# Expert weights of a mixture-of-experts layer: gate and up in steps of 1,024 columns over two PSUM banks, down with four consecutive rows to a partition

## The chip, the cores and the metric

The kernel runs on one core of a Trainium2 chip. The metric is the device time of one execution in microseconds (us); lower is better. The core has a matrix engine (TensorE: PE for its matrix products, PEld for the loads of its stationary operand), three engines for element-wise work (VectorE or DVE, ScalarE or ACT, GpSimd or POOL), and SyncE (SP), which here only issues DMA transfers. SBUF is the working memory with 128 partitions; PSUM, in eight banks of 128 x 512 floats, takes the results of PE.

## The reference, cut to what matters

The reference is two stacked networks over 256 tokens of 1,024 features in float32. The last stage, which takes more than half of the time, is a mixture of eight experts. Each token goes to its two best experts:

```python
for e in range(N_EXPERTS):                       # 8 experts
    h = jax.nn.silu(x @ w_gate[e]) * (x @ w_up[e])
    out = out + gates[..., e:e + 1] * (h @ w_down[e])
```

`w_gate[e]` and `w_up[e]` are 1,024 x 3,584, `w_down[e]` is 3,584 x 1,024. All three are float32, so the eight experts have 352 million bytes of weights (336 pieces of 2^20 bytes).

## The kernel before, in words

**Weights.** All weights go through one class, `Stream` (line 66). A unit is a piece of 128 partitions x 2,048 floats, 1 MB. `plan_experts` (line 1564) lists the units in the order of their use, and `_load` (line 90) issues one DMA on SP's queue for the next unit as soon as a raw buffer is free. In the expert stage there are some eleven raw buffers in several rings. `_split` (line 105) turns a unit into two float32r tiles: ACT casts it to the high part `wH` (line 122), and DVE subtracts that to get the low part `wL` (line 123). There are three buffers of `wH` and three of `wL`, and `get` (line 141) hands one unit over and splits up to two further ones ahead. A raw buffer is free again when DVE has read it.

**Products.** Each float32 product is made of three float32r ones, `mm3` (line 229, its matmuls are lines 231 to 233): high by high, high by low, low by high. The tokens of an expert are at most 128 slots, gathered into `xg[e]` (tiles of the tags `xg`, `hT` and `hH` in turn); they are the stationary operand, and 512 columns of a weight are the moving one.

**A step.** `experts` (line 1387) runs over 8 experts and 7 steps of 512 of the 3,584 columns. In a step, `up` (line 1403) makes the gate product (two units, 24 matmuls into one bank of the PSUM tag `mm`), ACT's silu of it into the tile `mh` (line 1406), the up product (two units, 24 matmuls, another bank of `mm`), and DVE's product of the two (line 1410). Then `down` (line 1422) multiplies the step before with two units of the down weight (24 matmuls into the two accumulator banks of the expert), and `turn` (line 1413) transposes the new `mh` in four pieces on PE (line 1416) into a bank of `mm` and splits the result into `mhH` (ACT, line 377) and `mhL` (DVE, line 380). `mm` has four banks, the accumulators another four (lines 1654 and 1655); `mh` has one buffer, `mhH` and `mhL` two each. One step is 72 matmuls of 512 columns and four transposes, on six units.

**What happens between experts.** After the first step of an expert, `y_parts` and `y_split` (lines 1455 and 1458) split the sum of the expert before into `hL`, two halves of 512. In its second step `slots_back` (line 1462) brings them back to the tokens with eight matmuls into four banks of `mm`, and `add_back` (line 1474) adds them to the output on DVE. During experts 1, 3 and 5 the tokens of the next two experts are gathered by `gather_steps` (line 1350): four calls with eight matmuls into one bank of `mm` each (line 1368) and four small splits, and a fifth with four matmuls (line 1379), in the steps n = 2 to 6:

```python
if e % 2 and e < N_EXP - 1 and n >= 2:
    if n == 2:
        steps = self.gather_steps([e + 1, e + 2], base)
    out = next(steps)
```

**Order.** The kernel's source gives priorities in program order; the framework's list scheduler then fixes one order for every engine ahead of the run, where an instruction that is not ready lets a later one pass, and assigns the buffers. The order within an engine does not change while the kernel runs. Loads are kept in program order.

**Weight loads.** A gate or up unit is four blocks of 128 rows by 512 columns (`u_k4n512`, line 164), so each partition receives four runs of 2 KB. A down unit is two blocks of 128 rows by all 1,024 columns (`u_k2n1024`, line 179), two runs of 4 KB to each partition.

Of the kernel before, what the change touches and what calls it, by code (L numbers as in the profile page):

```python
# [7 lines left out]
F32R = mybir.dt.float32r  # L8
I32 = mybir.dt.int32
AF = mybir.ActivationFunctionType  # L10
ALU = mybir.AluOpType
# [3 lines left out]
P = 128  # L15
DM = 1024
# [4 lines left out]
D_FF = 2816  # L21
N_EXP = 8
D_EXP = 3584

C_ID, C_INV, C_NH, C_EARLY = 0, 128, 130, 146
C_STRIU, C_IOTA, C_TIE, C_ID32, C_MAIN = 146, 274, 530, 594, 626
# [137 lines left out]
def u_k4n512(w, k0, n0, loads=1):  # L164
    def f(dst):
        m = 4 // loads
        return [(w[(k0 + k) * P:(k0 + k + m) * P, n0:n0 + 512].rearrange("(k p) n -> p k n", p=P),
                 dst[:, k * 512:(k + m) * 512].rearrange("p (k n) -> p k n", k=m)) for k in range(0, 4, m)]
    return f
# [6 lines left out]
    return f  # L176


def u_k2n1024(w, k0):
    def f(dst):  # L180
        return [(w[k0 * P:(k0 + 2) * P, :].rearrange("(k p) n -> p k n", p=P),
                 dst.rearrange("p (k n) -> p k n", k=2))]
    return f


# [7 lines left out]
class Kern:  # L193
# [1072 lines left out]
    def route(self, tt):  # L1266

        nc, c = self.nc, self.c
        mask, pos = self.rt
        if tt == 0:  # L1270
            self.logits = self.few(self.wr, N_EXP, self.mp, self.pair_end)
        l = self.rl[:, tt, :]
        tmp = self.t(self.mp, [P, 512], "mh", bufs=1)
        gt, eq = [tmp[:, i:i + 64].rearrange("p (i j) -> p i j", i=8) for i in (0, 64)]
        o = nc.vector.tensor_copy(l, self.logits[:, tt * 8:(tt + 1) * 8])
        if tt:
            self.tc.keep_in_program_order(o)
            self.behind(o, self.st.last[1])
        pin = self.tc.keep_in_program_order
        tie = c[:, C_TIE:C_TIE + 64].rearrange("p (i j) -> p i j", i=8)  # L1280
        lj = l[:, None, :].to_broadcast([P, 8, 8])
        li = l[:, :, None].to_broadcast([P, 8, 8])
        pin(nc.vector.tensor_tensor(eq, lj, li, op=ALU.is_equal))
        pin(nc.vector.tensor_tensor(eq, eq, tie, op=ALU.mult))
        pin(nc.vector.tensor_tensor(gt, lj, li, op=ALU.is_gt))
# [101 lines left out]
    def experts(self, st, base):  # L1387

        nc = self.nc
        mp = self.mp  # L1390
        xg, y = {}, {}

        def product(w, e):
            ps = self.mm()
            for kh in range(2):
                H, L = st.get(f"m{w}{e}")
                for kk in range(4):
                    k = kh * 4 + kk
                    s = slice(kk * 512, kk * 512 + 512)
                    self.mm3(ps, xg[e][0][:, k, :], xg[e][1][:, k, :], H[:, s], L[:, s], k == 0, k == 7)  # L1400
            return ps

        def up(e, n, dense, between):
            h = self.t(mp, [P, 512], "mh", bufs=1)
            if dense is None:
                nc.scalar.activation(h, product("g", e), AF.Silu)
                between()
            else:
                dense_gather(h, dense)
            nc.vector.tensor_tensor(h, h, product("u", e), op=ALU.mult)  # L1410
            return h

        def turn(h):
            ps = self.mm()
            for j in range(4):
                nc.tensor.transpose(ps[:, j * P:(j + 1) * P], h[:, j * P:(j + 1) * P], self.ident)
            H = self.t(mp, [P, 512], "mhH", F32R, bufs=2)
            L = self.t(mp, [P, 512], "mhL", F32R, bufs=2)
            self.split_to(H, L, ps)
            return H, L  # L1420

        def down(e, n, HL):
            aH, aL = HL
            if n == 0:
                y[e] = [self.acc() for _ in range(2)]
            for u in range(2):
                H, L = st.get(f"md{e}")
                for nh in range(2):
                    for kk in range(2):
                        a = slice((2 * u + kk) * P, (2 * u + kk + 1) * P)  # L1430
                        s = slice(kk * DM + nh * 512, kk * DM + nh * 512 + 512)
                        self.mm3(y[e][nh], aH[:, a], aL[:, a], H[:, s], L[:, s],
                                 n == 0 and u == 0 and kk == 0, n == 6 and u == 1 and kk == 1)

        def down_last(e, HL):

            yHL = y_parts()
            stats = [self.t(self.sp, [P, 2, 6], "bnst", bufs=4) for _ in range(2)]
            for nh in range(2):
                H, L = st.get(f"md{e}")  # L1440
                for kk in range(4):
                    if nh and kk == 3:
                        ps = slots_back(e, 0, yHL)
                    a, s = slice(kk * P, (kk + 1) * P), slice(kk * 512, (kk + 1) * 512)
                    self.mm3(y[e][nh], HL[0][:, a], HL[1][:, a], H[:, s], L[:, s], False, kk == 3)
# [41 lines left out]
        def dense_parts(ps):  # L1487
            HLs = []
            for tt in range(2):
                h = self.t(mp, [P, 512], "mh", bufs=1)  # L1490
                nc.scalar.activation(h, ps[tt], AF.Silu)
                HLs.append([self.t(mp, [P, 512], "mh" + c, F32R, bufs=2) for c in "HL"])
                self.split_to(*HLs[tt], h)
            return HLs

        def dense_gather(h, HLs):

            ps = self.mm()
            for tt in range(2):
                for i in range(2):  # L1500
                    nc.tensor.matmul(ps, self.oh[:, tt, 0, :], HLs[tt][i], start=tt + i == 0, stop=tt + i == 2)
            nc.scalar.copy(h, ps)

        dense = None
        if base == 0:
# [16 lines left out]
            rv = None  # L1522
        st.pieces = 1
        prev = None
        for e, n in [(e, n) for e in range(N_EXP) for n in range(7)]:
            if prev is None:
                h = up(e, n, dense, lambda: None)
                prev = (e, n, None, h)
                continue
            if prev[2] is None:  # L1530
                h0 = prev[3]
                turned = []
                h = up(e, n, None, lambda: turned.append(turn(h0)))
                prev = (0, 0, turned[0])
            else:
                h = up(e, n, None, lambda: None)
            if e and n == 1:
                for nh in range(2):
                    add_back(e - 1, nh, slots_back(e - 1, nh, yHL))
            down(*prev)  # L1540
            with self.soon(60 if st.i >= len(st.units) - 2 else 0):
                prev = (e, n, turn(h))
            if e and n == 0:
                yHL = y_parts()
                for nh in range(2):
                    y_split(e - 1, nh, yHL)
            if e % 2 and e < N_EXP - 1 and n >= 2:
                if n == 2:
                    steps = self.gather_steps([e + 1, e + 2], base)
                out = next(steps)  # L1550
                if out:
                    xg[e + 1], xg[e + 2] = out
        return rv, down_last(N_EXP - 1, prev[2])

    def rest(self):

# [7 lines left out]
    def plan_experts(self, st):  # L1564
        a = self.a
        wg, wu, wd = a["moe_w_gate_2"][0], a["moe_w_up_2"][0], a["moe_w_down_2"][0]

        def dn(e, n):
            for u in range(2):
                st.add(f"md{e}", u_k2n1024(wd[e], n * 4 + 2 * u))  # L1570

        def dn_last(e, n):
            for nh in range(2):
                st.add(f"md{e}", u_k4n512(wd[e], n * 4, nh * 512, nh + 1))

        prev = None
        for e in range(N_EXP):
            for n in range(7):
                for c, w in (("g", wg), ("u", wu)):
                    for kh in range(2):  # L1580
                        st.add(f"m{c}{e}", u_k4n512(w[e], 4 * kh, n * 512))
# [238 lines left out]
```

## Time and profile before

| what | us |
|---|---|
| median of 3 runs (1815.80 to 1818.71) | 1817.25 |
| the profiled execution | 1815.42 |
| its span, first to last instruction | 1813.3 |

The profile is of one execution. Its page gives busy time by engine, then the span in 40 slices, then groups of instructions; a matmul's duration there includes the time in which it overlaps its neighbours, so the distance between the starts of two matmuls is what one of them costs. The expert stage begins at about 820 us of the span and PE's last matmul is near 1799 us; a layer norm and the output follow to 1813 us. A wait is put down to the engine or the DMA whose semaphore came last.

### The profile page before, as it was taken

How to read it: one execution, taken by the hardware profiler on the slowest of the kernel's cores; microseconds unless marked ns; L12 is line 12 of the kernel's file. 1: busy time of each engine (PE TensorE's matmuls, PEld its weight loads, DVE VectorE, ACT ScalarE, POOL GpSimd, SP SyncE). 2: the span in 40 equal slices, each digit the busy share in tenths (PEclk: the TensorE clock that was granted, in tenths of full speed). 3: DMA queues.
4: the chain of work that ended last, by engine and by line, in shares of the span. 5: the costliest groups of instructions: out<-in, count | busy, mean ns of one | idle time of the engine just before them, and what ended most of it. 6: DMA issues, size and time to landing. Idle time of an engine off the chain costs nothing. (4 is left out here: it accounts for less than half of the span.)

```text
span 1813.3 us, 24175 instructions
## 1 busy us (share of the span) xinstructions
PE 1755.9 (97%) x9653; PEld 1476.9 (81%) x9653; DVE 1435.7 (79%) x1453; ACT 1064.9 (59%) x1008; POOL 74.7 (4%) x116
## 2 busy tenths in 40 slices
PE   6999999999999999999999999999999999999996
PEld 3888767889689998977888888888878888888885
DVE  3899576569775557679889899888898898888887
ACT  3334344646343333347777777777777767677674
POOL 1010013002100001000000000000000000000000
PEclk9999999999999999999999999999999999999998
DMA  9988445249265557547999999999999999999991
GB/s 349 318 305 311 161 152 179 66 132 309 68 201 192 183 191 251 174 158 295 358 363 364 357 356 359 372 360 358 345 343 375 372 347 355 349 368 369 355 370 47
DMA packets 252615, 509.34 MB, mean 281 GB/s; under 512 B 12347, under 2 KB 68782, under 8 KB 251470
## 3 DMA queue, kind: packets, MB, share of 16 engines
q1 hardware_dynamic: 249550, 500.64, 78.0%
q0 software_dynamic: 2592, 6.97, 1.2%
q8 instruction: 78, 1.28, 0.3%
q14 instruction: 43, 0.35, 0.1%
q10 hardware_dynamic: 352, 0.10, 0.0%
HBM read 504.28 MB, written 1.05 MB: 279 GB/s over the span
## 5 line engine op out<-in xcount | busy, mean ns | idle before, releaser
L123 DVE TENSOR_TENSOR wL<-raw,wH 128x2048 fp32r<-128x2048 f32 (+2 forms) x582 | 1032.3, 1799 | 193.2 <-ACT wH L122 187.7
L122 ACT CAST wH<-raw 128x2048 fp32r<-128x2048 f32 (+2 forms) x582 | 870.0, 1520 | 410.3 <-PE mm L232 128.0
L231 PE MATMUL mm<-hH,wH 128*128 128x256 f32 x816 | 231.8, 284 | 0.0
L232 PE MATMUL mm<-hL,wH 128*128 128x256 f32 x816 | 231.6, 284 | 0.0
L233 PE MATMUL mm<-hH,wL 128*128 128x256 f32 x816 | 231.2, 283 | 0.0
L231 PE MATMUL mm<-wH,hH 128*128 128x512 f32 (+1 forms) x512 | 197.1, 387 | 5.7 <-ACT wH L122 2.6
L232 PE MATMUL mm<-wL,hH 128*128 128x512 f32 (+1 forms) x512 | 197.6, 386 | 2.6 <-DVE wL L123 2.5
L232 PE MATMUL acc<-wL,mhH 128*128 128x512 f32 x448 | 176.8, 395 | 0.0
L233 PE MATMUL acc<-wH,mhL 128*128 128x512 f32 x448 | 174.7, 390 | 0.0
L231 PE MATMUL acc<-wH,mhH 128*128 128x512 f32 x448 | 162.6, 390 | 0.0
L231 PEld LDWEIGHTS mm<-hH,wH 128*128 128x128 f32 x816 | 156.5, 192 | 1.2 <-issue 0.8
L232 PEld LDWEIGHTS mm<-hL,wH 128*128 128x128 f32 x816 | 156.5, 192 | 0.4
L233 PEld LDWEIGHTS mm<-hH,wL 128*128 128x128 f32 x816 | 156.5, 192 | 0.1
L232 PE MATMUL mm<-wL,hT 128*128 128x512 f32 x336 | 131.9, 392 | 2.0 <-DVE wL L123 1.9
L232 PE MATMUL mm<-wL,xg 128*128 128x512 f32 x328 | 129.2, 394 | 3.6 <-DVE wL L123 3.5
L231 PE MATMUL mm<-wH,hT 128*128 128x512 f32 x336 | 131.4, 391 | 0.0
L233 PE MATMUL mm<-wH,hT 128*128 128x512 f32 x336 | 130.8, 389 | 0.0
L231 PE MATMUL mm<-wH,xg 128*128 128x512 f32 x328 | 128.8, 393 | 0.0
L233 PE MATMUL mm<-wH,xg 128*128 128x512 f32 x328 | 128.4, 392 | 0.2 <-DVE xg L380 0.2
L231 PEld LDWEIGHTS mm<-wH,hH 128*128 128x128 f32 x512 | 97.0, 190 | 25.5 <-ACT wH L122 5.3
L232 PEld LDWEIGHTS mm<-wL,hH 128*128 128x128 f32 x512 | 97.3, 190 | 23.5 <-DVE wL L123 5.5
L233 PE MATMUL mm<-wH,hL 128*128 128x512 f32 (+1 forms) x288 | 110.2, 383 | 0.8 <-DVE hL L380 0.7
(385 smaller groups left out, 2429.9 us busy)
## 6 DMA issues: line engine op xcount, KB each, us to landing
raw<-in_moe_w_gate_dram SPq DMA_DIRECT2D x112, 1024.0 KB
raw<-in_moe_w_up_dram SPq DMA_DIRECT2D x112, 1024.0 KB
raw<-in_moe_w_down_dram SPq DMA_DIRECT2D x111, 1024.0 KB
raw<-in_ret_w_in_dram SPq DMA_DIRECT2D x24, 1024.0 KB
raw<-in_mod_w_dram SPq DMA_DIRECT2D x32, 512.0 KB
raw<-in_fox_w_in_dram SPq DMA_DIRECT2D x16, 1024.0 KB
raw<-in_sc_w_in_dram SPq DMA_DIRECT2D x12, 1024.0 KB
raw<-in_ffn_w_gate_dram SPq DMA_DIRECT2D x11, 1024.0 KB
```

The costliest lines, as they stand in the source:

```text
L122: ops = (K.nc.scalar.copy(H[:, s], raw[:, s]), K.nc.vector.tensor_tensor(L[:, s], raw[:, s], H[:, s], op=ALU.subtract))
L123: K.nc.vector.tensor_tensor(L[:, s], raw[:, s], H[:, s], op=ALU.subtract))
L231: self.mm_first = mmul(ps, sH, mH, start=first, stop=False)
L232: mmul(ps, sH, mL, start=False, stop=False)
L233: self.mm_last = mmul(ps, sL, mH, start=False, stop=last)
```

## The change

The columns of an expert are cut into four steps instead of seven: 512, 1024, 1024, 1024 for the first expert and 1024, 1024, 1024, 512 for the others. In a step of 1,024 the gate product is four units of two row blocks by 1,024 columns, and goes to two banks of `mm` at once; so does the up product. The order of the matmuls alternates between the two banks after each `mm3`. `turn` makes two banks of transposes, and `down` takes four units. `mh` becomes 128 x 2 x 512. A down unit now holds, for each partition, two of four consecutive rows of the weight (8 KB in one run); for that the columns of the gate and up products are read from PSUM in the order "every fourth column" (`by_row`). The gather of the next experts' tokens now runs in the steps n = 0 to 3, with two calls in the last.

```diff
+def steps_of(e):
+    ws = [512, 1024, 1024, 1024] if e == 0 else [1024, 1024, 1024, 512]
+    return [(sum(ws[:i]), w) for i, w in enumerate(ws)]
...
-def u_k2n1024(w, k0):
+def u_k2n1024(w, k0, n0=0):
     def f(dst):
-        return [(w[k0 * P:(k0 + 2) * P, :].rearrange("(k p) n -> p k n", p=P),
+        return [(w[k0 * P:(k0 + 2) * P, n0:n0 + 1024].rearrange("(k p) n -> p k n", p=P),
...
+def u_rows(w, r0, j0, nj, n0, n1, loads=1):
+    def f(dst):
+        v = w[r0:r0 + 512, n0:n1].rearrange("(p j) n -> p j n", j=4)
+        m, c = nj // loads, n1 - n0
+        return [(v[:, j0 + i:j0 + i + m, :], dst[:, i * c:(i + m) * c].rearrange("p (j n) -> p j n", j=m))
+                for i in range(0, nj, m)]
+    return f
...
+        def by_row(ps):
+            return ps.rearrange("p (c j) -> p j c", j=4)
...
+        def product(w, e, n):
+            width = steps_of(e)[n][1]
+            b = width // 512
+            pss = [self.mm() for _ in range(b)]
+            m = 2048 // width
+            for u in range(8 // m):
                 H, L = st.get(f"m{w}{e}")
+                for kk in range(m):
+                    k = u * m + kk
+                    for i in range(b):
+                        s = slice(kk * width + i * 512, kk * width + i * 512 + 512)
+                        self.mm3(pss[i], xg[e][0][:, k, :], xg[e][1][:, k, :], H[:, s], L[:, s], k == 0, k == 7)
+            return pss
...
         def up(e, n, dense, between):
-            h = self.t(mp, [P, 512], "mh", bufs=1)
+            h = self.t(mp, [P, 2, 512], "mh", bufs=1)
+            hv = [h[:, i, :].rearrange("p (j c) -> p j c", j=4) for i in range(2)]
             if dense is None:
-                nc.scalar.activation(h, product("g", e), AF.Silu)
+                for v, ps in zip(hv, product("g", e, n)):
+                    nc.scalar.activation(v, by_row(ps), AF.Silu)
                 between()
...
+            for i, ps in enumerate(product("u", e, n)):
+                nc.vector.tensor_tensor(hv[i], hv[i], by_row(ps), op=ALU.mult)
+                hs.append(h[:, i, :])
...
-            if e % 2 and e < N_EXP - 1 and n >= 2:
-                if n == 2:
+            if e % 2 and e < N_EXP - 1:
+                if n == 0:
                     steps = self.gather_steps([e + 1, e + 2], base)
-                out = next(steps)
+                for _ in range(2 if n == 3 else 1):
+                    out = next(steps)
...
         def dn(e, n):
-            for u in range(2):
-                st.add(f"md{e}", u_k2n1024(wd[e], n * 4 + 2 * u))
+            r0, width = steps_of(e)[n]
+            for r in range(r0, r0 + width, 512):
+                for u in range(2):
+                    st.add(f"md{e}", u_rows(wd[e], r, 2 * u, 2, 0, DM))
```

## Rows read from the trace of the kernel before

**Rows 1.** The page: busy time by engine, then the share of the DMA engines.

```profile
PE 1755.9 (97%) x9653; PEld 1476.9 (81%) x9653; DVE 1435.7 (79%) x1453; ACT 1064.9 (59%) x1008; POOL 74.7 (4%) x116
...
DMA  9988445249265557547999999999999999999991
```

**Rows 2.** Busy time in stretches: us, by engine, PE's clock, DMA share, GB/s.

```profile
796.00:801.00 5.00, 4.96 (x27) 3.83 (x26) 3.50 (x6) 2.05 (x4) 0.00 (x0) 1.00 0.00 0
...
838.60:1797.00 958.40, 954.09 (x4348) 787.21 (x4346) 847.85 (x537) 696.40 (x500) 1.10 (x2) 1.00 0.97 351
```

**Rows 3.** Waits from 850 to 1800 us: who for whom, us, times, longest.

```profile
ACT wH L122 <- PE mm L233: 91.7, 139, 1.5
...
PEld mm L232 <- DVE wL L123: 9.4, 14, 1.2
...
DVE wL L123 <- DMA raw<-in_moe_w_gate_dram: 3.6, 4, 0.9
```

**Rows 4.** Waits of SP's own queue, 850 to 1800 us.

```profile
SPq L209 <- DVE wL L123: 724.2, 298, 5.0
```

**Rows 5.** PE's timeline: no DMA running, then in the expert stage.

```profile
799.16 0.39 PE L232 MATMUL mm<-wL,hH 128*128 128x512 f32 x1
799.38 0.39 PE L233 MATMUL mm<-wH,hL 128*128 128x512 f32 x1
799.61 0.39 PE L231 MATMUL mm<-wH,hH 128*128 128x512 f32 x1
...
899.60 0.49 PE L1416 MATMUL mm<-cst,mh 128*128 128x128 f32 x3
...
900.17 0.27 PE L1416 MATMUL mm<-cst,mh 128*128 128x128 f32 x1
...
916.39 0.49 PE L1416 MATMUL mm<-cst,mh 128*128 128x128 f32 x3
```

**Rows 6.** Groups by line and shape, 850 to 1800 us: count, busy us, mean ns.

```profile
L123 DVE TENSOR_TENSOR wL<-raw,wH 128x2048 fp32r<-128x2048 f32 x313 | 709.1, 2287 | 70.6 <-ACT wH L122 65.4 <-DMA raw<-in_moe_w_gate_dram 3.6 <-DMA raw<-in_moe_w_down_dram 0.4
...
L380 DVE TENSOR_TENSOR mhL<-mm,mhH 128x512 fp32r<-128x512 f32 x55 | 37.5, 682 | 1.3 <-ACT mhH L377 1.3
L1410 DVE TENSOR_TENSOR mh<-mh,mm 128x512 f32<-128x512 f32 x54 | 37.0, 685 | 26.3 <-PE mm L233 26.3
L1406 ACT ACTIVATE mh<-mm 128x512 f32<-128x512 f32 x54 | 32.4, 600 | 44.6 <-PE mm L233 44.6
...
L123 DVE TENSOR_TENSOR wL<-raw,wH 128x1024 fp32r<-128x1024 f32 x20 | 23.2, 1219 | 1.4 <-ACT wH L122 1.3
...
L122 ACT CAST wH<-raw 128x1024 fp32r<-128x1024 f32 x20 | 19.7, 1049 | 1.7 <-PE mm L233 1.7
```

**Rows 7.** PE's timeline at the first gather step of expert 1.

```profile
985.38 0.60 PE L1416 MATMUL mm<-cst,mh 128*128 128x128 f32 x4
985.73 0.36 PE L1368 MATMUL mm<-oh,xn 128*128 128x256 f32 x1
...
986.76 0.39 PE L231 MATMUL mm<-wH,hT 128*128 128x512 f32 x1
```

**Rows 8.** DVE's timeline at the same place.

```profile
987.52 2.29 DVE L123 TENSOR_TENSOR wL<-raw,wH 128x2048 fp32r<-128x2048 f32 x1 [0.43 <-ACT wH L122]
989.73 0.68 DVE L380 TENSOR_TENSOR mhL<-mm,mhH 128x512 fp32r<-128x512 f32 x1
```

**Rows 9.** PE's timeline at the change from expert 2 to expert 3.

```profile
1196.25 0.39 PE L231 MATMUL mm<-wH,xg 128*128 128x512 f32 x1
1197.37 0.50 PE L232 MATMUL mm<-wL,xg 128*128 128x512 f32 x1 [0.73 <-DVE wL L123]
```

**Rows 10.** DVE's timeline at the same place.

```profile
1193.21 0.69 DVE L380 TENSOR_TENSOR hL<-acc,hL 128x512 fp32r<-128x512 f32 x1 [0.30 <-ACT hL L377]
1193.82 0.68 DVE L380 TENSOR_TENSOR mhL<-mm,mhH 128x512 fp32r<-128x512 f32 x1
1195.02 2.29 DVE L123 TENSOR_TENSOR wL<-raw,wH 128x2048 fp32r<-128x2048 f32 x1 [0.52 <-ACT wH L122]
```

**Rows 11.** Packets of all DMA queues, 850 to 1800 us.

```profile
DMA packets 139646, 331.48 MB, mean 349 GB/s; under 512 B 5088, under 2 KB 5088, under 8 KB 139590
```

More of the change, by code (lines that the diff above doesn't have):

```diff
@@ L1272, in route @@
         l = self.rl[:, tt, :]
-        tmp = self.t(self.mp, [P, 512], "mh", bufs=1)
+        tmp = self.t(self.mp, [P, 2, 512], "mh", bufs=1)[:, 0, :]
         gt, eq = [tmp[:, i:i + 64].rearrange("p (i j) -> p i j", i=8) for i in (0, 64)]
@@ L1391, in experts @@
         xg, y = {}, {}
-        def product(w, e):
-            ps = self.mm()
-            for kh in range(2):
-                H, L = st.get(f"m{w}{e}")
[L1397 to L1401, printed above, removed]
+        def by_row(ps):
[6 more added lines that the diff above has]
+            for u in range(8 // m):
+                H, L = st.get(f"m{w}{e}")
+                for kk in range(m):
[4 more added lines that the diff above has]
+            return pss
@@ L1403, in up @@
         def up(e, n, dense, between):
-            h = self.t(mp, [P, 512], "mh", bufs=1)
+            h = self.t(mp, [P, 2, 512], "mh", bufs=1)
+            hv = [h[:, i, :].rearrange("p (j c) -> p j c", j=4) for i in range(2)]
             if dense is None:
-                nc.scalar.activation(h, product("g", e), AF.Silu)
+                for v, ps in zip(hv, product("g", e, n)):
+                    nc.scalar.activation(v, by_row(ps), AF.Silu)
                 between()
             else:
-                dense_gather(h, dense)
@@ L1410, in up @@
[L1410 to L1423, printed above, removed]
+                dense_gather(hv[0], dense)
@@ new lines, in up, with turn @@
+            hs = []
+            for i, ps in enumerate(product("u", e, n)):
+                nc.vector.tensor_tensor(hv[i], hv[i], by_row(ps), op=ALU.mult)
+                hs.append(h[:, i, :])
+            return hs
+        def turn(hs):
+            HLs = []
+            for h in hs:
+                ps = self.mm()
+                for j in range(4):
+                    nc.tensor.transpose(ps[:, j * P:(j + 1) * P], h[:, j * P:(j + 1) * P], self.ident)
+                HLs.append([self.t(mp, [P, 512], "mh" + c, F32R, bufs=2) for c in "HL"])
+                self.split_to(*HLs[-1], ps)
+            return HLs
@@ L1424, in down @@
+        def down(e, n, HLs):
             if n == 0:
                 y[e] = [self.acc() for _ in range(2)]
-            for u in range(2):
[L1427 to L1433, printed above, removed]
+            for i, (aH, aL) in enumerate(HLs):
+                for u in range(2):
+                    H, L = st.get(f"md{e}")
+                    for nh in range(2):
+                        for kk in range(2):
+                            a = slice((2 * u + kk) * P, (2 * u + kk + 1) * P)
+                            s = slice(kk * DM + nh * 512, kk * DM + nh * 512 + 512)
+                            self.mm3(y[e][nh], aH[:, a], aL[:, a], H[:, s], L[:, s],
+                                     n == 0 and i + u + kk == 0, n == 3 and i == len(HLs) - 1 and u + kk == 2)
@@ L1489, in dense_parts @@
             for tt in range(2):
-                h = self.t(mp, [P, 512], "mh", bufs=1)
+                h = self.t(mp, [P, 2, 512], "mh", bufs=1)[:, 0, :]
                 nc.scalar.activation(h, ps[tt], AF.Silu)
@@ L1501, in dense_gather @@
                     nc.tensor.matmul(ps, self.oh[:, tt, 0, :], HLs[tt][i], start=tt + i == 0, stop=tt + i == 2)
-            nc.scalar.copy(h, ps)
+            nc.scalar.copy(h, by_row(ps))
         dense = None
@@ L1524, in experts @@
         prev = None
-        for e, n in [(e, n) for e in range(N_EXP) for n in range(7)]:
+        for e, n in [(e, n) for e in range(N_EXP) for n in range(4)]:
             if prev is None:
@@ L1546, in experts @@
                     y_split(e - 1, nh, yHL)
-            if e % 2 and e < N_EXP - 1 and n >= 2:
-                if n == 2:
+            if e % 2 and e < N_EXP - 1:
+                if n == 0:
                     steps = self.gather_steps([e + 1, e + 2], base)
-                out = next(steps)
+                for _ in range(2 if n == 3 else 1):
+                    out = next(steps)
                 if out:
                     xg[e + 1], xg[e + 2] = out
-        return rv, down_last(N_EXP - 1, prev[2])
+        return rv, down_last(N_EXP - 1, prev[2][0])
     def rest(self):
@@ L1568, in dn @@
         def dn(e, n):
-            for u in range(2):
-                st.add(f"md{e}", u_k2n1024(wd[e], n * 4 + 2 * u))
+            r0, width = steps_of(e)[n]
+            for r in range(r0, r0 + width, 512):
+                for u in range(2):
+                    st.add(f"md{e}", u_rows(wd[e], r, 2 * u, 2, 0, DM))
         def dn_last(e, n):
             for nh in range(2):
-                st.add(f"md{e}", u_k4n512(wd[e], n * 4, nh * 512, nh + 1))
+                st.add(f"md{e}", u_rows(wd[e], steps_of(e)[n][0], 0, 4, nh * 512, nh * 512 + 512, nh + 1))
         prev = None
         for e in range(N_EXP):
-            for n in range(7):
+            for n, (n0, width) in enumerate(steps_of(e)):
                 for c, w in (("g", wg), ("u", wu)):
-                    for kh in range(2):
-                        st.add(f"m{c}{e}", u_k4n512(w[e], 4 * kh, n * 512))
+                    if width == 512:
+                        for kh in range(2):
+                            st.add(f"m{c}{e}", u_k4n512(w[e], 4 * kh, n0))
+                    else:
+                        for u in range(4):
+                            st.add(f"m{c}{e}", u_k2n1024(w[e], 2 * u, n0))
                 if prev is not None:
```

## The prediction

> **What bounds the kernel now.** I read the page first: PE is busy for 97% of the span and DVE for 79%, and from the middle on the DMA engines show nines too [rows 1]. So two resources look full at once, and the question is which of them sets the pace of the expert stage. The busy times by stretch say the same of the stage alone: in 958.4 us PE is busy for 954.1, DVE for 847.9, ACT for 696.4, and the DMA share is 0.97 [rows 2].
>
> The waits decide it. ACT waits for PE to give back a split buffer, 91.7 us in 139 waits; DVE waits for landing gate weights in four places, 3.6 us in all [rows 3]. On SP's queue the loads wait for a raw buffer that DVE has to read first, 724.2 us in 298 waits, of the 950 us looked at [rows 4]. The loads are held back by their consumers, so the nines are a queue that is served as fast as it is emptied. PE is the bound.
>
> How much of PE's time is left? With no DMA running at all, matmuls of 512 columns start 0.22 to 0.23 us apart [rows 2, 5]. In the expert stage a whole step, from one group of transposes to the next, takes 916.39 - 899.60 = 16.79 us [rows 5]. It holds 72 matmuls and 4 transposes. I take 0.227 us for a matmul, and 16.79 - 72 x 0.227 = 0.45 us remain, 0.11 for each transpose. So a step has no idle time, and a matmul costs the same beside a full DMA queue as without one. What PE loses in the stage are the waits for `wL`: 9.4 us in 14 waits at the weight loads [rows 3], mostly where one expert follows another. There PE stands from 1196.25 to 1197.37, 0.9 us over a normal distance [rows 9], because DVE had two more 0.68 us splits in its queue ahead of a unit [rows 10]. These 9.4 us are nearly all that a change of this stage's order can give back.
>
> **The change, part by part.** *Matmuls and transposes.* 4,032 matmuls of 512 columns (56 x 72) and 224 transposes before and after; only their grouping changes: 0.
>
> *Larger packets.* The number of loads and their size stay (336 units of 1 MB, on SP's queue, in order); 139,646 packets [rows 11] become fewer, since gate and up runs go from 2 to 4 KB in the wide steps, down runs from 4 to 8 KB. What hides their time is PE, as shown; if that cover were gone, it is the rival below. 0. The Trainium skill (Perfetto Trace Analysis, section DMA Optimizations) says that going from 2 KB to 4 or 8 KB can improve throughput dramatically and calls it the primary step for a kernel bound by DMA. By that rule the sum would be the one of the second faster rival below; rows 3 and 4 do not show its condition here.
>
> *Silu, product, splits.* Per 512 columns the same: a silu of 0.600 us, a product of 0.685, an `mhL` split of 0.682 [rows 6]. They now come in pairs. A unit leaves DVE 12 x 0.227 - 2.287 = 0.44 us free; the second of a pair costs 0.69 more at once, which two units take up. Two units are split ahead, and four units of down follow before the transposes: 0.
>
> *Reading every fourth column of PSUM.* No row shows such a read. A gain is excluded, since the same elements are read; the nearest row from above is one with twice the elements, 1,219 ns on DVE and 1,049 on ACT against 685 and 600 [rows 6], so at most 0.53 and 0.45 us for each 512 columns. On DVE a wide step would then pay 2 x 0.53 = 1.07 us at once, and the four down units that follow leave 4 x 0.44 = 1.8. I take 0, as the shapes are those of the contiguous rows; the upper end, if nothing is absorbed, is 24 wide steps x 1.07 = 26 us. The Trainium skill (PSUM — Partial Sum Buffer, section Specifications (TRN2)) speaks against such reads, if for matmuls: PSUM's lines have 8 bytes, and a pattern that is not contiguous slows matmuls significantly. Nothing measured here shows whether that reaches ACT and DVE; if it did in full, the sum would be the +26 us of the upper end.
>
> *PSUM banks at the gather steps.* This is where I see a new wait. Before, a step needs gate, up, transposes and gather: four banks of `mm`, just what there are. Now at the end of a wide step two banks hold transposes and one the gather's sums, and the next gate product asks for two more: five of four. The second must wait until the first bank of transposes is split, that is for `mhL` on DVE. In the trace the first gate matmul behind a gather step starts at 986.76 [rows 7], and that split ends at 989.73 + 0.68 = 990.41, as DVE had a unit of weights ahead of it [rows 8]: 3.65 us later. Four more transposes move the gate's start by 0.45, so 3.2 us must be covered. The matmuls of the first bank can cover them where the scheduler puts them first: of two units already split they are 2 x 6 x 0.227 = 2.72 us, and 0.5 is left. If the order stays as written, only three matmuls (0.68 us) come first and 2.5 us is left; if a third unit is ready, nothing. There are 12 such places (experts 1, 3, 5, four steps). I take 12 x 0.5 = +6 us, as two units ahead is what the split buffers hold; ends 0 and 30.
>
> *Changes of expert.* One more pair of splits stands in the burst that now makes PE wait, and at experts 1, 3 and 5 the first gather step has moved into it. That is at most 0.68 us at each of seven changes, 4.8 in all; on the other side the waits could go, -9.4. I take 0, since twice as many units now lie between the burst and the `slots_back` that needs it, and keep both ends. `slots_back` and `add_back` move by no instruction.
>
> *First step.* Behind the 512-wide first step of expert 0, gate, transposes and up ask for five banks once, and the single `mh` makes the silu wait for the transposes: at most some 3 us, once; I take 0. POOL's queue and SP's order of issue lose or gain nothing.
>
> The sum: +6 us. The profiled execution took 1815.42 us, 2.1 over its span and 1.8 under the median of the runs, so it becomes 1821.4, and the median 1817.25 + 6 = **1823 us**.
>
> **The rivals.** *No change that shows.* All of the gather's waits are covered by the first bank's matmuls and the bursts by the split buffers, so the step keeps its 16.79 us: 1817. For it: a step is already without idle time, and PE's work is the same. Against it: five banks of four.
>
> *Faster: the waits for `wL` go.* Twice as many units between two bursts give DVE time to get ahead, and the changes of expert no longer stop PE. The place is the first gate product of an expert [rows 9]; the point is whether DVE has two pairs of splits in its queue there or three, against the 0.44 us that each unit frees. Price: up to -9.4, so 1808 to 1813. Against it: the burst itself grows.
>
> *Faster, because loads set the pace.* If the DMA share near 1 [rows 1] were the limit, fewer packets would shorten every step. But PE's own distance of 0.227 leaves nothing beyond those same 9.4 us, so the time is again no less than 1808. Rows 3 and 4 speak against it, and its chance is a small part of that of the rival above. It is what the rule of the Trainium skill named above would do here.
>
> *Clearly slower: the order stays as written, or the strided reads take double.* 12 x 2.5 = 30 us, or up to 26: 1840 to 1850. For it: the order is fixed ahead of the run, so PE cannot choose another instruction when a bank is late. Against it: the fixed order does fill gaps with other work, as the fourth transpose at 900.17 shows, which stands 0.57 us behind the start of the other three with a matmul between [rows 5].
>
> **How the numbers follow.** About 0.2% (3.6 us) is what a measurement of this kernel can tell from no change. I give the forecast (+4 to +15) 0.34, no change 0.32, the two faster cases together 0.24, the clearly slower one 0.10. So faster 0.24, same 0.32, slower 0.44. As cases of both signs hold most of the chance, the forecast's own range is 1821 to 1832. The whole range goes from 1809 (most of the 9.4 us gained) to 1840 (the forecast with the upper ends of the change of expert and the first step, and the begin of the clearly slower case); it leaves out some 0.15.
>
> **What would show it.** Right, if in the changed profile PE waits for DVE's `mhL` behind the gather of experts 1, 3 and 5, with some 0.5 us each, while between these an undisturbed wide step takes 2 x 16.33 + 8 x 0.11, near 33.6 us. The silu and product should keep 0.60 and 0.69 us; if they read 1.0 to 1.2, the strided reads cost. Packets should fall to some six tenths and the DMA share of the stage below 0.97 with no gain in time; if the stage gets shorter by more than 10 us, the matmul's distance has changed, and my reading of PE as the bound is wrong. The waits for `wL` in total say who wins at the changes of expert.

## The result and the profile after

The changed kernel takes 1832.7 us (median of 4 runs, 1830.43 to 1834.42) against 1817.5 for the kernel before, run beside it: a ratio of 1.0087, 95% interval 1.0074 to 1.0100, so about 15 us slower. The profiled execution took 1832.41 us, its span is 1830.2; the one of before had 1815.42 and 1813.3. In the two traces PE's first product of the expert stage starts within 1 us of the same time and its last matmul 16.8 us later than before, so the whole loss lies in the expert stage.

The page of the changed kernel, busy time by engine and the share of the DMA engines, looks like the one of before [rows 1]:

```profile
PE 1763.9 (96%) x9653; PEld 1474.3 (81%) x9653; DVE 1439.9 (79%) x1453; ACT 1065.2 (58%) x1008; POOL 74.7 (4%) x116
...
DMA  9989545239255557548999999999999999999991
```

Busy time and clock in the stretch that answers to the second of [rows 2] (the columns are the same):

```profile
838.60:1814.00 975.40, 961.84 (x4352) 784.84 (x4350) 853.03 (x538) 696.39 (x501) 1.10 (x2) 1.00 0.94 345
```

The clock is full in both and ACT has the same work, 696.4 us. PE has 975.4 - 961.8 = 13.6 us without work in its records, against 4.3 before. Its busy time grew as well, by 7.8 us for the same matmuls, partly because their starts lie further apart behind a wait. The waits say for whom. This view is that of [rows 3], of 850 to 1817 us (who for whom, us, times, longest):

```profile
ACT wH L129 <- PE mm L250: 92.6, 117, 1.5
...
DVE wL L130 <- ACT wH L129: 76.7, 107, 2.9
...
ACT mh L1434 <- PE mm L250: 50.2, 23, 3.0
...
PEld mm L249 <- DVE wL L130: 25.6, 40, 1.4
...
DVE wL L130 <- DMA raw<-in_moe_w_gate_dram: 6.6, 10, 2.9
```

PE's weight loads wait for `wL` 25.6 us instead of 9.4, and DVE for `wH` 76.7 us. One row is new in kind: the silu's wait for the gate product is up to 3.0 us long. In the kernel before none was over 1.6:

```profile
ACT mh L1406 <- PE mm L233: 44.6, 54, 1.6
```

SP's queue still waits for raw buffers, 743.8 us in 297 waits [rows 4]:

```profile
SPq L226 <- DVE wL L130: 743.8, 297, 6.3
```

The groups by shape that answer to [rows 6], 850 to 1815 us (count, busy us, mean ns, idle before): the weight subtraction, the split of the transposes, the product and the silu. The last two now read every fourth column of PSUM and cost what they did, 685 and 599 ns:

```profile
L130 DVE TENSOR_TENSOR wL<-raw,wH 128x2048 fp32r<-128x2048 f32 x313 | 710.4, 2290 | 88.4 <-ACT wH L129 74.2 <-DMA raw<-in_moe_w_gate_dram 6.6 <-DMA raw<-in_moe_w_up_dram 2.6
...
L397 DVE TENSOR_TENSOR mhL<-mm,mhH 128x512 fp32r<-128x512 f32 x55 | 37.4, 685 | 2.1 <-ACT mhH L394 2.0
...
L1440 DVE TENSOR_TENSOR mh<-mh,mm 128x512 f32<-128x512 f32 x55 | 36.6, 685 | 9.8 <-PE mm L250 9.8
L1434 ACT ACTIVATE mh<-mm 128x512 f32<-128x512 f32 x53 | 31.8, 599 | 51.6 <-PE mm L250 50.2
```

The packets fell to 57% of [rows 11], for nearly the same bytes (331.8 MB against 331.5):

```profile
DMA packets 79832, 331.84 MB, mean 343 GB/s; under 512 B 5090, under 2 KB 5090, under 8 KB 65952
```

**Where the time went.** PE's timeline shows eleven waits of 0.96 us for `wL`, the first at 1139.34, the last at 1765.24, all in the first or third step of experts 2 to 7. One of them:

```profile
1194.88 0.61 PE L248 MATMUL mm<-wH,xg 128*128 128x512 f32 x2
1196.45 0.50 PE L249 MATMUL mm<-wL,xg 128*128 128x512 f32 x1 [0.96 <-DVE wL L130]
```

The second matmul of the first row starts at 1194.88 + 0.23 = 1195.11 and the next one at 1196.45: 1.35 us instead of 0.227, so 1.12 us are lost, 12.3 in eleven. Why is `wL` late? ACT's timeline, at the end of the gate product of that step (start, duration, what; in brackets the idle time before it and what ended it):

```profile
1186.92 1.92 ACT L129 CAST wH<-raw 128x2048 fp32r<-128x2048 f32 x1 [0.80 <-PE mm L250]
1191.68 0.60 ACT L1434 ACTIVATE mh<-mm 128x512 f32<-128x512 f32 x1 [2.84 <-PE mm L250]
1192.17 1.90 ACT L129 CAST wH<-raw 128x2048 fp32r<-128x2048 f32 x1
1193.97 0.60 ACT L1434 ACTIVATE mh<-mm 128x512 f32<-128x512 f32 x1
```

ACT stands 2.84 us until the first bank of the gate product is complete, makes the first silu, and only then the cast of the unit two ahead, which stands behind it in ACT's fixed order. DVE waits as long for that cast:

```profile
1188.87 2.29 DVE L130 TENSOR_TENSOR wL<-raw,wH 128x2048 fp32r<-128x2048 f32 x1 [0.43 <-DMA raw<-in_moe_w_gate_dram]
1194.11 6.78 DVE L130 TENSOR_TENSOR wL<-raw,wH 128x2048 fp32r<-128x2048 f32 x3 [2.94 <-ACT wH L129]
```

Its subtraction ends 2.29 us later at 1196.40, and PE goes on at 1196.45. In the kernel before no step up to the last expert has the silu ahead of such a cast. In the changed one a cast stands between the two silus in 15 of the 24 wide steps (an early silu, below): eleven are the places of the waits, and four are second steps of an expert, where two matmuls start 0.50 to 0.53 us apart (at 1112, 1363, 1614 and 1738).

### The profile page after: what moved, and what is told of

Same layout as the page of the kernel before. It is cut to its first block, busy times and chain, and to the rows that moved or that the text cites. A ratio compares the mean times of both kernels' runs of the same rounds, so it can differ in the third digit from the quotient of the medians.

```text
span 1830.2 us, 24195 instructions
## 1 busy us (share of the span) xinstructions
PE 1763.9 (96%) x9653; PEld 1474.3 (81%) x9653; DVE 1439.9 (79%) x1453; ACT 1065.2 (58%) x1008; POOL 74.7 (4%) x116
## 5 line engine op out<-in xcount | busy, mean ns | idle before, releaser
L248 PE MATMUL mm<-hH,wH 128*128 128x256 f32 x816 | 231.8, 284 | 0.0
L248 PE MATMUL mm<-wH,hH 128*128 128x512 f32 (+1 forms) x512 | 190.4, 387 | 5.7 <-ACT wH L129 2.6
L248 PE MATMUL acc<-wH,mhH 128*128 128x512 f32 x448 | 161.3, 390 | 0.0
L248 PEld LDWEIGHTS mm<-hH,wH 128*128 128x128 f32 x816 | 156.6, 192 | 1.2 <-issue 0.8
L250 PE MATMUL mm<-wH,hT 128*128 128x512 f32 x336 | 131.1, 391 | 0.0
L250 PE MATMUL mm<-wH,xg 128*128 128x512 f32 x328 | 128.8, 393 | 0.2 <-DVE xg L397 0.2
L248 PE MATMUL mm<-wH,hT 128*128 128x512 f32 x336 | 123.2, 391 | 0.2 <-ACT wH L129 0.2
L248 PE MATMUL mm<-wH,xg 128*128 128x512 f32 x328 | 121.3, 393 | 1.2 <-ACT mh L1523 1.2
L248 PEld LDWEIGHTS mm<-wH,hH 128*128 128x128 f32 x512 | 96.9, 190 | 25.8 <-ACT wH L129 5.3
```

Source lines behind the costliest of these rows:

```text
L248: self.mm_first = mmul(ps, sH, mH, start=first, stop=False)
L250: self.mm_last = mmul(ps, sL, mH, start=False, stop=last)
```

## The experiments

The medians of the experiments stand against those of the kernel before, run beside them (1817.8 to 1818.0) and, where that is said, against the 1832.7 of the changed kernel.

**1. The silu behind the cast.** One line of `up`. `behind(a, b)` puts a after b in the fixed order, without a semaphore, and `st.last[0]` is the cast of the unit that was split last, here the one two ahead:

```diff
-                    nc.scalar.activation(v, by_row(ps), AF.Silu)
+                    self.behind(nc.scalar.activation(v, by_row(ps), AF.Silu), st.last[0])
```

> The changed kernel, with the silu of the gate product held behind the weight cast that is two units ahead, on ACT's queue. Theory (order on ACT): in eleven wide steps of experts 2 to 7 the fixed order of ACT has the first silu ahead of one more weight cast, so that the cast waits for the end of the gate product, DVE's wL comes late, and PE stands 1.35 us from start to start instead of 0.227. With the order turned round these eleven gaps go, 11 x 1.1 = 12 us: 1820 to 1822, and the waits of the second matmul of a product for wL fall from 25.6 us to about 13. Rival (the bursts of paired splits on DVE, or the PSUM banks, make PE wait, and the order on ACT only follows): the gaps move to another matmul and the time stays at 1831 to 1834.

Measured: 1816.36 us, ratio to the kernel before 0.9991 (0.9981 to 1.0002). The whole loss is gone, 16.3 us against the changed kernel. ACT's timeline at the same step (this profile runs 1187.26 - 1186.92 = 0.34 us later there):

```profile
1187.26 1.92 ACT L129 CAST wH<-raw 128x2048 fp32r<-128x2048 f32 x1 [0.80 <-PE mm L250]
1189.97 1.91 ACT L129 CAST wH<-raw 128x2048 fp32r<-128x2048 f32 x1 [0.80 <-PE mm L250]
1192.02 1.28 ACT L1434 ACTIVATE mh<-mm 128x512 f32<-128x512 f32 x2
```

The cast that stood at 1192.17 now starts at 1189.97, which is 2.5 us earlier with the 0.34 us by which this profile runs later, and the first silu at 1192.02 - 0.34 = 1191.68 is no later than it was. The waits of PE for `wL` (weight loads, then matmuls) are:

```profile
PEld mm L249 <- DVE wL L130: 7.9, 20, 0.8
```

```profile
PE mm L249 <- DVE wL L130: 2.1, 6, 0.4
```

That is below the 9.4 us of the kernel before [rows 3], and none of the waits of 0.96 us is left. The theory named 1820 to 1822 and got 4 us more. The two traces say where they come from: from its first gate matmul to that of the next expert, expert 3 with two long waits takes 127.45 us in the changed kernel and 124.94 here, 1.25 for each; expert 4 with two long waits and one of the four smaller places takes 123.90 and 120.79, so the smaller one costs 0.6. Eleven times 1.25 and four times 0.6 are 16.2 us. The rival, that the gaps would move to another matmul, falls.

**2. Half of it.** The same, in the third step of each expert only: `n == 2 and self.behind(o, st.last[0])`, with `o` the silu. Six places of the 15, six of the eleven long waits.

> The changed kernel, with the silu held behind the weight cast in the third step of each expert alone, which is 6 of the 15 places (and 6 of the eleven long gaps) of the first experiment. Theory (each early silu has a price of its own): 6 gaps of 1.12 us go and 5 stay; by the first experiment's 16.5 us over 15 places, or over eleven gaps, 6.6 to 9 us less than the changed kernel, 1823.5 to 1826. Rival (one late unit drags the next along, so that either all go or none): 1816 or 1832.

Measured: 1824.59 us, ratio 1.0044 (1.0030 to 1.0059), 8.1 us less than the changed kernel, and five waits of 0.96 us are left in the trace. 8.1 / 6 = 1.35 us for each place; the places add up one by one. In the expert stage the order on PE and on DVE is that of the changed kernel, instruction for instruction, and ACT's alone differs, so nothing else in the order can have given this back.

**3. The other way: early silus everywhere.** In all 24 wide steps the cast is held behind the first silu, `self.behind(st.last[0], o)`.

> The changed kernel, with the weight cast held behind the first silu of the gate product in all 24 wide steps; in the changed kernel it already stands there in 15 of them, so nine steps more, in experts 0, 1, 3 and 5. Theory (the early silu makes PE wait): 9 x 1.1 to 1.4 us = 10 to 13 us more, 1842 to 1846, and new gaps of 1.35 us in experts 0 and 1. Rival (DVE is ahead there, or the gap was a matter of experts 2 to 7 alone): 1831 to 1835.

Measured: 1838.5 us, ratio 1.0114 (1.0098 to 1.0129), 5.8 us more than the changed kernel, not 10 to 13. The direction is right: there are 16 waits of 0.96 us now, the five new ones in experts 0 to 2, and one of 1.52 us in expert 0. One of the five:

```profile
876.43 0.61 PE L248 MATMUL mm<-wH,xg 128*128 128x512 f32 x2
878.00 0.50 PE L249 MATMUL mm<-wL,xg 128*128 128x512 f32 x1 [0.96 <-DVE wL L130]
```

But only six of the nine new places stop PE: the second steps of experts 1, 3 and 5 do not. The second step is the one that holds `slots_back`, eight matmuls more on PE, 8 x 0.227 = 1.8 us, and in this kernel's order four of them stand in a row ahead of the matmul that needs the late `wL` in expert 3 (at 1233.38, 0.44 us from start to start). That these give ACT and DVE the time is the likely reason; it was not tried by itself. The order on PE and DVE moved with this edit in other places too, so its price is less clean than that of experiment 2.

**4. The same fault in the kernel before.** Steps of 512, nothing of the change, the cast held behind the silu in the first and the fifth step of experts 2 to 7 (the expectation says eleven steps; the edit makes it twelve):

```diff
-                nc.scalar.activation(h, product("g", e), AF.Silu)
+                o = nc.scalar.activation(h, product("g", e), AF.Silu); e > 1 and n in (0, 4) and self.behind(st.last[0], o)
```

> The kernel before, steps of 512, with the weight cast held behind the silu in eleven steps (the first and the fifth step of experts 2 to 7, but for one); nothing of the change is in it. Theory (the price of the change is the order on ACT, not the width): the silu is ready only at the end of the whole gate product, 0.68 us later than the first of a pair, so a gap is 1.1 to 1.8 us, 12 to 20 us in all: 1830 to 1838. Rival (narrow steps absorb it, and it is the pair of silus that makes PE wait): 1816 to 1820.

Measured: 1837.07 us, ratio 1.0112 (1.0098 to 1.0127): 19.2 us more, 1.6 for each of twelve steps. ACT and PE at the first of them:

```profile
1063.22 0.60 ACT L1406 ACTIVATE mh<-mm 128x512 f32<-128x512 f32 x1 [3.45 <-PE mm L233]
1063.71 5.50 ACT L122 CAST wH<-raw 128x2048 fp32r<-128x2048 f32 x3
```

```profile
1065.74 0.42 PE L231 MATMUL mm<-wH,hH 128*128 128x512 f32 x1
1067.46 0.73 PE L231 MATMUL acc<-wH,mhH 128*128 128x512 f32 x2 [1.29 <-ACT wH L122]
```

ACT idles 3.45 us instead of 2.84, as the one silu needs the end of the whole gate product, and PE stands 1.72 us from start to start. So the width of the steps is not what costs; the order is, in either kernel.

**5. The gather's sums in accumulator banks.** `steps = self.gather_steps([e + 1, e + 2], base, bank=self.acc)`, so that a gather step needs four banks of `mm`.

> The changed kernel, with the gather's sums in accumulator banks instead of the banks of the products, so that a gather step asks for four banks of mm and no longer for five. Forecast's theory (the fifth bank is waited for): 6 us less, 1826 to 1827. Rival (the scheduler covers the bank, as no wait for mhL stands behind a gather in the changed kernel's trace): no change beyond 2 us, 1831 to 1834, or a shift either way of a few gaps of 1.1 us, if the order around them falls otherwise.

Measured: 1832.83 us, ratio 1.0077 (1.0061 to 1.0093), the changed kernel's time. The fixed order shifted a little with the edit (nine of the 0.96 us waits, 17 early silus), so the better comparison is the same edit on top of experiment 1, without any early silu:

> The first experiment's kernel, with the gather's sums in accumulator banks as well, so that a gather step asks for four banks of mm and not five, with the early silus out of the way. Forecast's theory (the fifth bank is waited for, hidden so far by the larger gaps): up to 6 us less than the first experiment, 1810 to 1812. Rival (the splits of the transposes come ahead of the next weight unit on DVE, so the bank is back in time): within 2 us of the first experiment, 1814 to 1818.

Measured: 1816.82 us, ratio 0.9995 (0.9986 to 1.0004), where experiment 1 has 0.9991. The order around the gathers moved in this kernel as well, but the fifth bank costs nothing that shows.

**6. The gather later.** No gather call in an expert's first step, one in the second, two in the third and in the fourth.

> The changed kernel with the gather of the next two experts kept out of the first step of an expert: one call in the second step, two in the third and two in the fourth. Theory (order on ACT): the eleven gaps stand in experts 2 to 7 whether these gather or not, so they stay unless the scheduler's order happens to fall otherwise: 1829 to 1834. Rival (the gather step in the burst at the change of expert costs): up to 0.7 us at each of three changes, and with the bank wait of four steps' worth up to 6 us less, 1826 to 1830.

Measured: 1835.78 us, ratio 1.0101 (1.0085 to 1.0117), nothing gained, eleven waits of 0.96 us still there. And at one place, in expert 1, where two gather calls follow a wide step (two banks of transposes and two of sums, so the next gate product finds no bank at all), the forecast's wait appears. PE, then DVE:

```profile
1036.99 0.28 PE L1385 MATMUL mm<-oh,x 128*128 128x256 f32 x1
1039.43 0.50 PE L248 MATMUL mm<-wH,hT 128*128 128x512 f32 x1 [2.15 <-DVE mhL L397]
```

```profile
1036.48 2.29 DVE L130 TENSOR_TENSOR wL<-raw,wH 128x2048 fp32r<-128x2048 f32 x1 [0.42 <-ACT wH L129]
1038.69 0.68 DVE L397 TENSOR_TENSOR mhL<-mm,mhH 128x512 fp32r<-128x512 f32 x1
```

DVE has a unit of weights ahead of the split, and PE stands until the split gives back the bank. The mechanism exists; the change does not set it off.

**7. The old layout of the down weights, contiguous reads.** `by_row` takes the columns as they stand, and down units are the two row blocks of before:

```diff
-            return ps.rearrange("p (c j) -> p j c", j=4)
+            return ps.rearrange("p (j c) -> p j c", j=4)
...
-                    st.add(f"md{e}", u_rows(wd[e], r, 2 * u, 2, 0, DM))
+                    st.add(f"md{e}", u_k2n1024(wd[e], r // P + 2 * u))
```

(The last step's down units change in the same way.)

> The changed kernel with the old layout of the down weights (rows 128 apart, runs of 4 KB) and contiguous reads of PSUM in silu and product; the steps stay 1,024 wide and the order on all engines but SP's addresses stays the same. Theory (order on ACT): neither the strided reads nor the packets cost or give anything, 1831 to 1834 as the changed kernel, silu 0.60 and product 0.685 us. Rival (every-fourth-column reads or the 8 KB runs have a price that the durations don't show): over 4 us less or more; the upper end of the forecast for the reads was 26 us less.

Measured: 1833.29 us, ratio 1.0091 (1.0076 to 1.0106), the changed kernel's time. The order on PE, DVE and ACT is unchanged by the edit, so this is a clean comparison: the 8 KB runs and the reads of every fourth column together make no difference that shows.

**8. Two attempts at a version faster than both.** First the change of expert: on top of experiment 1, `y_split` is called behind the silu of the next expert's second step, for both halves or for the second alone.

> The first experiment's kernel, with both splits of an expert's output sums (hL) moved from the end of the next expert's first step to behind the silu of its second one, so that they leave the burst at the change of expert. Theory (the burst of splits on DVE makes PE wait for wL there): the gaps of 0.71 to 0.80 us at seven changes of expert go, 7 x 0.5 = 3.5 us less than the first experiment: about 1813, under both kernels by some 0.25%. Rival (the splits are late for the slots_back that reads them in the same step, or sit before the product there): 1816 to 1822.

> As the run before, with the second of the two splits moved alone. Theory: 0.68 us of DVE and 0.59 us of ACT leave the burst, which is about what PE lacks at a change (0.5 us), so most of the gaps go: 1813 to 1815. Rival (the move does not matter, or the second half is late for slots_back): 1816 to 1820.

Measured: 1816.94 and 1816.58 us, ratios 0.9998 (0.9988 to 1.0008) and 0.9995 (0.9985 to 1.0005), no gain over experiment 1. But neither kernel tests the theory, since the call moved and the splits did not: at all seven changes of expert both casts of `hL` stand in the fixed order ahead of that silu, in the burst as before. At the change to expert 4, with both calls moved (the silu of this step follows at 1343.86), ACT, then DVE:

```profile
1331.57 0.59 ACT L394 CAST hL<-acc 128x512 fp32r<-128x512 f32 x1 [0.89 <-PE acc L250]
1332.05 1.91 ACT L129 CAST wH<-raw 128x2048 fp32r<-128x2048 f32 x1
```

```profile
1333.99 2.29 DVE L130 TENSOR_TENSOR wL<-raw,wH 128x2048 fp32r<-128x2048 f32 x1 [1.12 <-ACT wH L129]
```

PE goes on at 1336.34, when this `wL` is ready; the distance there is 0.71 us, and at the changes to experts 2, 6 and 7 it is 0.71 to 0.73. What moved is mainly DVE's second split, which comes some 3 us later, and at the changes to experts 3 and 5 the distance fell from 0.79 us to 0.50 and 0.51. In the rows above DVE is idle for 1.12 us until ACT's cast, and that cast stands behind one of `hL` which waits for PE's sum of the expert before: it looks like the same fault as the early silu's, at another instruction. No run here holds that cast ahead, so this is read from the rows and not shown.

Then the start of the stage: on top of experiment 1 the routing's exponential is held behind the first wide step, so that ACT loads no table between the two silus of the dense part.

> The first experiment's kernel, with the routing's exponential moved behind the first wide step of expert 0, so that no table is loaded between the two silus of the dense part (in that kernel a load of 1.28 us at 830.21, behind which PE stands 1.6 us at 830.56). The rest is the same. Theory: 1.3 to 3 us less than the first experiment, 1813 to 1815, under both kernels. Rival (the two table loads cost as much at their new place, or PE waits for the next thing there): 1816 to 1818.

Measured: 1819.32 us, ratio 1.0003 (0.9990 to 1.0016), no gain. The load is gone from that place and another wait has taken it, for `wL`. PE's timeline, and the stretches before and after it with the columns of [rows 2]:

```profile
832.30 0.50 PE L1537 MATMUL mm<-mhL,oh 128*128 128x512 f32 x1 [0.22 <-DVE rmx L1361]
834.55 0.80 PE L249 MATMUL mm<-wL,xg 128*128 128x512 f32 x1 [1.75 <-DVE wL L130]
835.15 0.63 PE L250 MATMUL mm<-wH,xg 128*128 128x512 f32 x1
835.58 0.63 PE L249 MATMUL mm<-wL,xg 128*128 128x512 f32 x1
```

```profile
832.50:834.50 2.00, 0.30 (x1) 0.00 (x0) 2.00 (x3) 1.30 (x2) 0.00 (x0) 1.00 0.00 0
834.50:838.00 3.50, 3.44 (x8) 2.77 (x9) 3.50 (x5) 0.00 (x0) 0.00 (x0) 0.51 0.37 75
```

No version was found that beats both kernels by more than the measurement can tell; experiment 1 is as fast as the kernel before.

## Why the prediction was right and wrong

The forecast of 1823 us, slower, has the right sign, and 1832.7 lies in the whole range of 1809 to 1840, a little above the forecast's own of 1821 to 1832. But that is luck: its +6 us came from a wait that is not there, and the 15 us come from a term that it had put at nothing.

**The bound: right.** PE's distance of 0.227 us and the loads held back by buffers stand. An undisturbed wide step takes 33.59 us (first silu to first silu, 872.22 to 905.81), where the prediction had near 33.6. The DMA share fell from 0.97 to 0.94 without a gain.

**Larger packets, 0: right.** 57% of the packets, the same bytes, no gain; experiment 7 takes the 8 KB runs back (93,774 packets) and finds the same time. The prediction set the rule of the Trainium skill (Perfetto Trace Analysis, section DMA Optimizations), that larger transfers are the primary step for a kernel bound by DMA, against [rows 3, 4]. The runs side with the rows: the DMA engines were full because they were emptied no faster.

**Every fourth column, 0: right.** 599 and 685 ns, and experiment 7 gives nothing back. The Trainium skill (PSUM — Partial Sum Buffer, section Specifications (TRN2)) says of matmuls that a pattern that is not contiguous slows them significantly; no run here shows a matmul with such a pattern, and for the reads of ACT and DVE the durations rule a slowdown out.

**PSUM banks at the gather steps, +6: wrong, 0 measured.** The step that failed is the cover: "of two units already split they are 2 x 6 x 0.227 = 2.72 us, and 0.5 is left". The late bank is there once, as in [rows 8]. Behind the second gather call of expert 1, DVE has a unit of weights ahead of the split, and PE does not stand:

```profile
999.97 0.47 PE L248 MATMUL mm<-wH,hT 128*128 128x512 f32 x1
...
1003.38 0.40 PE L250 MATMUL mm<-wH,hT 128*128 128x512 f32 x1
1003.61 0.63 PE L248 MATMUL mm<-wH,hT 128*128 128x512 f32 x2
```

```profile
1000.70 2.29 DVE L130 TENSOR_TENSOR wL<-raw,wH 128x2048 fp32r<-128x2048 f32 x1 [0.42 <-ACT wH L129]
1002.90 0.68 DVE L397 TENSOR_TENSOR mhL<-mm,mhH 128x512 fp32r<-128x512 f32 x1
```

The split ends at 1002.90 + 0.68 = 1003.58, 3.6 us behind the first gate matmul, about the 3.65 of the prediction. From 999.97 on PE runs fifteen matmuls, five whole `mm3` one after the other, and only then two of L248 in a row. The rows do not name the bank, but five `mm3` of the first bank ahead of the second's are what fits: they cover 3.6 us and not 2.72. That is the prediction's own end of "nothing". Behind the first call of expert 1 the order is another, DVE takes the pair of splits first:

```profile
963.47 0.40 PE L248 MATMUL mm<-wH,hT 128*128 128x512 f32 x1
```

```profile
963.27 1.28 DVE L397 TENSOR_TENSOR hL<-acc,hL 128x512 fp32r<-128x512 f32 x2
964.47 1.46 DVE L397 TENSOR_TENSOR mhL<-mm,mhH 128x512 fp32r<-128x512 f32 x2
...
966.17 2.28 DVE L130 TENSOR_TENSOR wL<-raw,wH 128x2048 fp32r<-128x2048 f32 x1
```

The first split ends near 964.47 + 0.73 = 965.2, 1.7 us behind the first gate matmul. In experts 3 and 5 the gather's matmuls are spread among others, and the first split has ended before the next gate product starts. At none of the twelve places does a matmul wait for `mhL`. So the order of one place was taken for all twelve, although it is made anew for every version, and at the place where it came again the cover was longer. Experiment 5 shows the price, and experiment 6 what it would have been, 2.15 us at a place.

**Silu, product and splits in pairs, 0: wrong, and this is where the 15 us are.** This is the step that failed for the result. The prediction costed them by DVE's time alone ("Two units are split ahead, and four units of down follow before the transposes: 0"). It asked whether the engines have room for the work, and did not ask what is queued behind the silu on ACT while it waits for a product of now four units. That is the cast of the next unit but one, and a cast that comes 2.5 us late makes `wL` late, on a path where PE has two units in hand. The Trainium skill (PSUM — Partial Sum Buffer, section Engine vs sequencer instructions) calls ScalarE's queue strictly first in, first out; the trace agrees, as ACT idles 2.84 us with that cast behind the silu, though the cast could start 2.5 us earlier in experiment 1. Experiments 1 to 4 show it from four sides: taken away everywhere, in six places, added in nine, and added to the kernel before.

**Changes of expert, 0: right by size, with the wait misread.** Distances of 0.71 to 0.80 us stay at six of the seven changes, where [rows 9] had 1.12 from start to start; the waits for `wL` are 7.9 us in experiment 1 against 9.4. There was less to win than the prediction had: the 9.4 us are waits of the weight loads, and in the kernel before the matmuls themselves waited 4.1 us for `wL`. And the prediction misread [rows 10]. It put the wait down to "two more 0.68 us splits" ahead of a unit in DVE's queue, but those end at 1193.82 + 0.68 = 1194.50, and DVE is then idle for 0.52 us until ACT's cast. ACT's timeline in the kernel before:

```profile
1192.59 0.59 ACT L377 CAST hL<-acc 128x512 fp32r<-128x512 f32 x1 [0.58 <-PE acc L233]
1193.07 1.91 ACT L122 CAST wH<-raw 128x2048 fp32r<-128x2048 f32 x1
```

The cast stands behind an instruction that waits for PE, as behind the early silu; what it would give to hold it ahead was not tried. So a late cast on ACT already stood in the rows that the prediction had.

**First step, 0: right.** What PE's matmuls of expert 0 take above 0.227 us sums to 6.0 us in the trace of before and 6.1 in that of after.

**The rivals.** "Clearly slower, the order stays as written" is the nearest: the cause is an order fixed ahead of the run, at 1.25 us for each long wait. But it put this on PE and the banks; PE's order around the gather was good, and the one on ACT was not, and the time is below this rival's 1840. "No change that shows" is what the change is worth once that order is mended: 1816.36 us.

**What stays open.** Why the framework's scheduler puts the silu first in 15 steps and not in the other nine. It decides by its own estimate of when things are ready, and the two silus of a pair are ready 3 matmuls (0.68 us) apart, where before there was one; experiment 7 shows that the layout of the down weights and the reads have no part in it, as the order is the same there. Beyond that it was not tried.

## What to carry to other kernels

Where the order of an engine is fixed ahead of the run, ask of every instruction that waits what stands behind it on its own engine and who is fed by that: an engine with 40% of its time free still stopped the bound one, for 15 us. After a change to the structure compare the new order with the old, pairs of neighbours first, before costing the work itself; one explicit dependency gave back all that the change had lost. And a row of the old order (who stood ahead of whom) is no price for the new one. Where a row names what ended a wait, start from that and not from what stood before it.

## What the runs showed of the hardware that was not expected

In the run with the later exponential PE had started one matmul in the 2.25 us from 832.30 to 834.55; the granted clock of the stretch behind it is 0.51, the lower level of 1.2 GHz, and the matmuls there start 0.43 us apart instead of 0.227. The kernel before does the same at the start of the stage: 0.61 from 830 to 834 us, behind 4 us in which PE was busy for 1.91. So a stand can be followed by a second cost, after it is over. But the length of one stand does not decide it. In experiment 6 PE stood for 2.43 us from start to start (1036.99 to 1039.43) in the middle of the stage, and the granted clock of 1039.4 to 1044 is 1.00; the twelve stands of about 1.7 us of experiment 4 and the eleven of 1.35 of the changed kernel left it at 1.00 too. What tells the places apart was not tried.
